# First norm's squares shared by two engines and summed on TensorE block by block, with the conditioning rows spread between them

## The chip, the cores and the metric

The kernel runs on one core of a Trainium2 chip. The metric is device time in microseconds (us) of one execution; of the kernel before there are three, with a median of 1330.14 us (1330.12 to 1335.97). A further execution was taken with the hardware profiler; all durations below come from it.

Engine names are those of the profile: PE is TensorE's matmul, PEld its weight load, DVE is VectorE, ACT is ScalarE, POOL is GpSimd, SP is SyncE, which here only issues DMAs. Each engine works through its own instructions in the order in which they were issued; engines wait for each other through semaphores.

## The reference

Two layers of a hybrid diffusion backbone: 256 latent tokens and 256 context tokens of width 1024. Each layer is an RMSNorm with a shift and a scale that depend on a conditioning vector, a combined projection into three token mixers, gates, a residual, a second such norm, a SwiGLU and a residual. What matters here is the beginning of the first layer:

```
silu_c, silu_cc = silu(c), silu(c_ctx)
mx = (silu_c @ w_ada[l] + b_ada[l])          # 6 rows of 1024: shift, scale, gate, ...
y = x * rsqrt(mean(x * x, axis=-1) + 1e-6) * g
h = y * (1 + scale) + shift                  # then h @ w_in
```

Every token needs the sum of 1024 squares before the first projection can begin. The context tokens use `silu_cc` in place of `silu_c`.

## The kernel before

All activations are kept transposed: eight tiles `h[0]` to `h[7]`, each 128 features (partitions) by 512 tokens (256 context, then 256 latent) in float32. They come in as four DMAs of two tiles each (`h_tiles`, L94). Weights come as a stream of 128x1024 blocks (`raw`, three buffers); ACT rounds each block to a high part and DVE computes the low part (L132, L122, tile `hl`), and every product is made of three matmuls (`mm3`, L204 to L206).

The order of the work is the order of the Python program: nothing is scheduled by a planner, and each engine's queue holds its instructions as the program issues them. The function that matters is `start()`. It does four things on the way to the first projection:

- **Conditioning rows (L483 to L489).** The two vectors `silu(c_ctx)` and `silu(c)` are spread over all partitions: 16 matmuls of 128x128 in float32 write four PSUM banks `outs[0..3]`, and `spread(i)` copies each bank into half of `cb[0]` or `cb[1]`. `cb` is used much later, by VectorE.
- **Norm sum (L491 to L502).** ACT squares each `h[k]` into a tile `sq` (four buffers), DVE adds it to `acc`, and when all eight are added four matmuls with a one-column operand (`acc` is the stationary side, `ones[:, 0:1]` the moving side) sum over the partitions: L502 writes four columns of bank `outs[4]`.
- **Shift and scale.** `nat_first(k)` multiplies the conditioning vectors with a block of weights (`wn`, L466), `nat_copy` takes the result out of PSUM, `nat_second(k)` turns it round (L476) and DVE makes the per-feature scale and shift `Ag` and `mods` (L477, L479).
- **Norm factor.** `norm_rstd` (L290 on ACT, L291, L292 and `newton` L272 to L274 on DVE) makes 1/rms, `norm_bcast` (L298) spreads it over the partitions into bank `outs[6]`, `mult` (L514) applies it, `mod` (L520 to L523) applies scale and shift and splits the result into `hn[k]`.

After that a loop over `k` runs seven output blocks per step (`block`, L531) on PE, with `nat_first(k + 1)` ahead of them.

In float32 the profile shows two passes for one matmul, each with its own weight load: the 16 matmuls of L486 are 32 instructions, the 4 of L502 are 8.

Of the kernel before, what the change touches and what calls it, by code (L numbers as in the profile page):

```python
# [12 lines left out]
AF = mybir.ActivationFunctionType  # L13
ALU = mybir.AluOpType
# [4 lines left out]
KT = 8  # L19
# [13 lines left out]
def hybrid_dit_kernel(ctx: ExitStack, tc: tile.TileContext, hT, wst, adaf, adan, vec_d,  # L33
                      bias_d, mask_d, dtab_d, rope_d, icnt_d, pw_d, out):
    nc = tc.nc
    V, S, P, TE = nc.vector, nc.scalar, nc.gpsimd, nc.tensor
# [10 lines left out]
    def pg():  # L47
        return pbank("g", 4)

    def pS():  # L50
        return pbank("s", 2)

    def pT():
        return pbank("t", 1)

    def pO():
        return pbank("o", 1)

    def tmp():
        return sm.tile([128, 512], F32, name="tmp", tag="tmp", bufs=3)  # L60
# [5 lines left out]
    ident = con.tile([128, 128], F32, name="ident")  # L66
    ones = con.tile([128, 64], F32, name="ones")
# [4 lines left out]
    cb = [con.tile([128, 1024], F32, name=f"cb{i}", tag=f"cb{i}") for i in range(2)]  # L72
# [11 lines left out]
    h = []  # L84
# [191 lines left out]
    def sqrt_table():  # L276
        S.activation(tiny(1, "dummy"), eps, AF.Sqrt)
# [10 lines left out]
    def norm_rstd(o, n):  # L288
        ms, sq, y = tiny(n, "ms"), tiny(n, "sq"), tiny(n, "rstd")
        S.activation(sq, o[:, :n], AF.Sqrt, bias=eps, scale=1.0 / D)  # L290
        V.tensor_scalar(ms, o[:, :n], 1.0 / D, 1e-6, op0=ALU.mult, op1=ALU.add)  # L291
        V.reciprocal(sq, sq)  # L292
        newton(y, sq, ms, n)
        return y

    def norm_bcast(y, tiles, R):
        for i, t in enumerate(tiles):
            TE.matmul(R[:, t * 128:(t + 1) * 128], y[:, i:i + 1].to_broadcast([128, 128]), ident,  # L298
                      start=True, stop=True)
        return R  # L300

# [7 lines left out]
    class Mod:  # L309
        def __init__(self, l, j, R, streams, share=True):  # L310
            self.a, self.t, self.k, self.share = (l, j, R, streams), None, 0, share

        def first(self, k):
            l, j, R, streams = self.a
            t = tmp()
            for s in streams:
                c = (CTX, X)[s]
                V.scalar_tensor_tensor(t[:, c], h[k][:, c], Ag[l][:, j, k, s:s + 1], R[:, c],
                                       op0=ALU.mult, op1=ALU.mult)
                b = mods[l][:, 24 * j + k, s:s + 1]  # L320
                if self.share and k % 2:
                    S.activation(t[:, c], t[:, c], AF.Identity, bias=b)
                    S.copy(hn[k][0][:, c], t[:, c])  # L323
                else:
                    S.activation(hn[k][0][:, c], t[:, c], AF.Identity, bias=b)  # L325
            return t
# [40 lines left out]
    def new_acc():  # L367
        return sm.tile([128, 512], F32, name="acc", tag="acc", bufs=1)
# [63 lines left out]
    def start():  # L432
        with tc.tile_pool(name="st", bufs=1) as sp:
# [4 lines left out]
            P.memset(ones, 1.0)  # L438
            S.activation(tiny(1, "dummy"), eps, AF.Silu)

            acc = new_acc()
            wn = {}

            def nat_load(k):
# [8 lines left out]
            csil = sp.tile([128, 8, 32], F32, name="csil")  # L453
# [6 lines left out]
            outs = [pg() for _ in range(4)] + [pS(), pS(), pT(), pO()]  # L460
            nat = outs[7]

            def nat_first(k):
                for kb in range(8):
                    g = slice(32 * (kb % 4), 32 * (kb % 4) + 32)
                    TE.matmul(nat[g, :256], csil[:, kb], wn[k][:, kb], start=(kb < 4), stop=(kb >= 4))  # L466

            def nat_copy():
                t = sp.tile([128, 256], F32, name="wt", tag="wt", bufs=2)
                V.tensor_copy(t, nat[:, :256])  # L470
                return t
# [8 lines left out]

            for s, off in enumerate((V_CC, V_C)):
                S.activation(csil[:, :, s], vec[:, off:off + 8], AF.Silu)
            for i in range(4):  # L483
                for b in range(4):
                    kb = 4 * (i % 2) + b
                    TE.matmul(outs[i][:, b * 128:(b + 1) * 128], csil[:, kb, i // 2:i // 2 + 1].to_broadcast([128, 128]),  # L486
                              ident, start=True, stop=True)
            def spread(i):
                S.copy(cb[i // 2][:, (i % 2) * 512:(i % 2) * 512 + 512], outs[i])  # L489

            for k in range(KT):  # L491
                t = sp.tile([128, 512], F32, name="sq", tag="sq", bufs=4)
                S.activation(t, h[k], AF.Square)
                if k == 0:
                    V.tensor_copy(acc, t)
                else:
                    V.tensor_tensor(acc, acc, t, op=ALU.add)
            sqrt_table()
            spread(0)
            o = outs[4]  # L500
            for i in range(4):
                TE.matmul(o[:, i:i + 1], acc[:, i * 128:(i + 1) * 128], ones[:, 0:1], start=True, stop=True)  # L502
            nat_first(0)
            y = norm_rstd(o, 4)
            for i in range(1, 4):
                spread(i)
            R = norm_bcast(y, range(4), outs[6])
            t0 = nat_copy()
            prep_to(0, True)
            Rs = sp.tile([128, 512], F32, name="Rs")  # L510
# [1 line left out]
            def mult(k):  # L512
                t = tmp()
                V.tensor_tensor(t, h[k], R if k == 0 else Rs, op=ALU.mult)  # L514
                return t
# [9 lines left out]
            t = mult(0)  # L525
# [8 lines left out]
            for k in range(KT):  # L534
# [3 lines left out]
                if more:  # L538
                    nat_first(k + 1)
                    prep_to(k + 1, True)  # L540
                    t = mult(k + 1)
# [688 lines left out]
    with tc.manual_schedule():  # L1230
        outs, u = start()
        with tc.tile_pool(name="mx0", bufs=1) as mp:
            ada_units(0, (2, 3, 4, 5), (0, 1))
            mixer(0, mp, outs, u)
        with tc.tile_pool(name="ff0", bufs=1) as fp:
            outs = out_ffn(0, fp)
        with tc.tile_pool(name="mx1", bufs=1) as mp:
            mixer(1, mp, outs, None)
        with tc.tile_pool(name="ff1", bufs=1) as fp:
            out_ffn(1, fp)  # L1240
# [119 lines left out]
```

## Time and profile before

| | |
|---|---|
| median of the runs | 1330.14 us |
| profiled execution, whole | 1340.45 us |
| its span on the core | 1338.7 us |
| PE busy | 1313.8 us (98%) |
| DVE busy | 850.1 us (64%) |
| ACT busy | 582.0 us (43%) |
| mean granted clock of PE | 0.99 |

The profiled execution is 10.31 us longer than the median of the others, so a difference is worked out against its 1340.45 us and then carried to the median. Busy shares are averages over the whole span. The change lies in the first 22 us, and there they say little: what counts is the chain of work that leads to the first projection. The profile's column for the granted clock has 1.00 for 2.4 GHz and 0.50 for 1.2 GHz; before the first recorded change of the clock it prints 1.00.

### The profile page before, as it was taken

The page shows a single profiled execution, that of the slowest core. Times are in us where ns is not written, and L with a number is a line of the kernel's source. Part 1 is how long each engine was busy: PE and PEld are TensorE (multiplying, and loading weights), DVE is VectorE, ACT ScalarE, POOL GpSimd, SP SyncE. Part 2 cuts the span into 40 slices and gives each one's busy share as a digit, 9 for nine tenths or more (in the row PEclk, how much of TensorE's full clock was granted, in tenths as well). Part 3 has the DMA queues.
Part 4 walks back from the last instruction along what each step waited for, and adds up shares of the span by engine and source line. Part 5 has one row for each costly group of instructions (what it writes and reads, how often), then busy time and mean ns, then how long its engine had stood idle before and what let it go on. Part 6 is the DMA issues. An engine that isn't in the chain of part 4 may idle for free.

```text
span 1338.7 us, 19983 instructions
## 1 busy us (share of the span) xinstructions
PE 1313.8 (98%) x7842; PEld 1145.4 (86%) x7842; DVE 850.1 (64%) x1445; ACT 582.0 (43%) x902; POOL 144.4 (11%) x213
## 2 busy tenths in 40 slices
PE   7999999999999999999999999999999999999997
PEld 6787777888888888888888888988889999999997
DVE  4487462877877666566565553665647887655554
ACT  4455555452232434222122232465567545643453
POOL 0034131111000010000000000152242200000000
PEclk7999999999999999999999999999999999999999
DMA  8433312443554514444445653142426775455552
GB/s 311 163 128 124 106 57 86 149 135 127 172 174 166 196 64 143 150 162 159 157 142 176 206 185 110 58 152 97 151 95 220 239 270 185 158 188 189 189 175 95
DMA packets 60141, 207.79 MB, mean 155 GB/s; under 512 B 6800, under 2 KB 11280, under 8 KB 59024
## 3 DMA queue, kind: packets, MB, share of 16 engines
q1 hardware_dynamic: 48528, 164.58, 36.4%
q10 hardware_dynamic: 11520, 41.95, 9.2%
q8 instruction: 61, 1.00, 0.3%
q14 instruction: 32, 0.26, 0.1%
HBM read 205.45 MB, written 1.05 MB: 154 GB/s over the span
## 4 chain that ended last, share of the span: by engine, by line
PE 86%; DVE 6%; ACT 4%; DMA 2%; issue 1%; SPq 0%; ACTq 0%; POOL 0%; DVEq 0%
PE pg L204 26%; PE pg L206 26%; PE pg L205 26%; DMA raw<-in_wst 1%; DVE hl L122 1%; ACT hl L132 1%; PE pt L687 1%; PE po L699 1%; PE po L909 1%; PE ps L656 1%; PE ps L655 1%; PE po L466 1%; DVE tmp L393 1%; DMA h<-in_hT 0%; ACT hn L325 0%
## 5 line engine op out<-in xcount | busy, mean ns | idle before, releaser
L204 PE MATMUL pg<-hn,hl 128*128 128x256 f32 (+1 forms) x1568 | 524.7, 335 | 2.7 <-ACT hn L325 1.1
L206 PE MATMUL pg<-hn,hl 128*128 128x256 f32 (+1 forms) x1568 | 520.5, 332 | 0.5 <-POOL hn L334 0.4
L205 PE MATMUL pg<-hn,hl 128*128 128x256 f32 (+1 forms) x1568 | 519.6, 331 | 0.9 <-DVE hl L122 0.9
L122 DVE TENSOR_TENSOR hl<-raw,hl 128x1024 fp32r<-128x1024 f32 (+1 forms) x277 | 342.8, 1243 | 157.8 <-ACT hl L132 157.0
L132 ACT CAST hl<-raw 128x1024 fp32r<-128x1024 f32 (+1 forms) x277 | 288.0, 1043 | 214.0 <-PE pg L206 98.1
L204 PEld LDWEIGHTS pg<-hn,hl 128*128 128x128 f32 x1568 | 296.4, 189 | 35.9 <-issue 3.8
L205 PEld LDWEIGHTS pg<-hn,hl 128*128 128x128 f32 x1568 | 297.8, 190 | 30.6 <-DVE hl L122 1.6
L206 PEld LDWEIGHTS pg<-hn,hl 128*128 128x128 f32 x1568 | 296.1, 189 | 30.7 <-POOL hn L334 1.5
L393 DVE CUSTOM_DVE_ANT_0 tmp<-ada,cb 128x1024 bf16<-128x1024 f32 x128 | 155.6, 1223 | 25.7 <-DMA ada<-in_adaf 19.1
L204 PE MATMUL pg<-fh,hl 128*128 128x256 f32 (+1 forms) x374 | 122.0, 326 | 0.0
L205 PE MATMUL pg<-fh,hl 128*128 128x256 f32 (+1 forms) x374 | 121.8, 326 | 0.0
L206 PE MATMUL pg<-fh,hl 128*128 128x256 f32 (+1 forms) x374 | 121.8, 326 | 0.0
L306 ACT CAST fh<-sg 128x512 fp32r<-128x512 f32 (+1 forms) x44 | 22.6, 514 | 139.8 <-DVE sg L1158 139.8
L334 POOL TENSOR_TENSOR hn<-tmp,hn 128x256 fp32r<-128x256 f32 x20 | 14.8, 741 | 621.5 <-ACT hn L323 364.3
L205 PEld LDWEIGHTS pg<-fh,hl 128*128 128x128 f32 x374 | 71.1, 190 | 6.0
L204 PEld LDWEIGHTS pg<-fh,hl 128*128 128x128 f32 x374 | 70.4, 188 | 6.1
L206 PEld LDWEIGHTS pg<-fh,hl 128*128 128x128 f32 x374 | 70.4, 188 | 6.0
L350 DVE SCALAR_TENSOR_TENSOR h<-pg,mods,h 128x256 f32<-128x256 f32 x72 | 32.7, 480 | 64.1 <-PE pg L206 63.9
L204 PE MATMUL pg<-naq,hl 128*128 128x512 f32 (+1 forms) x192 | 64.5, 336 | 0.2 <-ACT tmp L1014 0.2
L206 PE MATMUL pg<-naq,hl 128*128 128x512 f32 (+1 forms) x192 | 64.1, 334 | 0.0
L205 PE MATMUL pg<-naq,hl 128*128 128x512 f32 (+1 forms) x192 | 64.0, 333 | 0.0
L1158 DVE TENSOR_TENSOR sg<-pg,sg 128x512 f32<-128x512 f32 (+1 forms) x44 | 24.5, 557 | 49.5 <-PE pg L206 46.1
(239 smaller groups left out, 1449.3 us busy)
## 6 DMA issues: line engine op xcount, KB each, us to landing
raw<-in_wst SPq DMA_DIRECT2D x277, 512.0 KB, 3.8
ada<-in_adaf ACTq DMA_DIRECT2D x80, 512.0 KB, 4.1
wn<-in_adan SPq DMA_DIRECT2D x8, 1024.0 KB, 7.1
h<-in_hT SPq DMA_DIRECT2D x8, 512.0 KB, 6.0
bm<-in_bias SPq DMA_DIRECT2D x32, 128.0 KB, 2.0
out<-yt SPq DMA_DIRECT2D x4, 256.0 KB, 2.0
cs<-in_rope SPq DMA_DIRECT2D x2, 256.0 KB, 3.1
pw<-in_pw SPq DMA_DIRECT2D x2, 256.0 KB, 3.9
```

Of the source, the lines that this page charges most:

```text
L122: V.tensor_tensor(t[:, 1, c], r[:, c], t[:, 0, c].bitcast(F32), op=ALU.subtract)
L132: S.copy(t[:, 0, width(j)], r[:, width(j)])
L204: TE.matmul(o, wh, xh, start=a, stop=False)
L205: TE.matmul(o, wl, xh, start=False, stop=False)
L206: TE.matmul(o, wh, xl, start=False, stop=z)
L306: S.copy(d0, src)
L334: P.tensor_tensor(hn[k][1][:, c], t[:, c], hi, op=ALU.subtract)
L350: V.scalar_tensor_tensor(h[k][:, c], o, mods[l][:, col + k, s:s + 1], h[k][:, c], op0=ALU.mult, op1=ALU.add)
L393: V.tensor_tensor_reduce(out=tmp().bitcast(BF16), in0=tiles[n], in1=cb[s], scale=1.0, scalar=0.0, op0=ALU.mult, op1=ALU.add, accum_out=mod ...
L466: TE.matmul(nat[g, :256], csil[:, kb], wn[k][:, kb], start=(kb < 4), stop=(kb >= 4))
L655: TE.matmul(o, naq[hd][:, qc], nakd[hd][:, kc], start=True, stop=False)
L1158: V.tensor_tensor(e["s"][:, c], o, e["s"][:, c], op=ALU.mult)
```

## The change

Four things are different, all in `start()`:

1. The even `h[k]` are squared on ACT, the odd ones on DVE. There is no `acc` and no addition on DVE.
2. Each square is summed by its own four one-column matmuls, which accumulate over the eight blocks in `outs[4]`: 32 matmuls in place of 4.
3. The 16 matmuls that spread the conditioning vectors are no longer issued together: five come first, one after each block's sum, three after the last.
4. `cb[1]` is copied by DVE in place of ACT, and all four copies are issued behind `norm_bcast`.

```diff
-            acc = new_acc()
...
-            for i in range(4):
-                for b in range(4):
+            rows = [(i, b) for i in range(4) for b in range(4)]
+
+            def spread_mm(n):
+                for i, b in rows[:n]:
                     kb = 4 * (i % 2) + b
-                    TE.matmul(outs[i][:, b * 128:(b + 1) * 128], csil[:, kb, i // 2:i // 2 + 1].to_broadcast([128, 128]),
-                              ident, start=True, stop=True)
+                    TE.matmul(outs[i][:, b * 128:(b + 1) * 128],
+                              csil[:, kb, i // 2:i // 2 + 1].to_broadcast([128, 128]), ident, start=True, stop=True)
+                del rows[:n]
+
             def spread(i):
-                S.copy(cb[i // 2][:, (i % 2) * 512:(i % 2) * 512 + 512], outs[i])
-
+                c = cb[i // 2][:, (i % 2) * 512:(i % 2) * 512 + 512]
+                if i < 2:
+                    S.copy(c, outs[i])
+                else:
+                    V.tensor_copy(c, outs[i])
+
+            o = outs[4]
+            spread_mm(5)
             for k in range(KT):
                 t = sp.tile([128, 512], F32, name="sq", tag="sq", bufs=4)
-                S.activation(t, h[k], AF.Square)
-                if k == 0:
-                    V.tensor_copy(acc, t)
+                if k % 2:
+                    V.tensor_tensor(t, h[k], h[k], op=ALU.mult)
                 else:
-                    V.tensor_tensor(acc, acc, t, op=ALU.add)
+                    S.activation(t, h[k], AF.Square)
+                for i in range(4):
+                    TE.matmul(o[:, i:i + 1], t[:, i * 128:(i + 1) * 128], ones[:, 0:1],
+                              start=(k == 0 and i == 0), stop=(k == KT - 1 and i == 3))
+                spread_mm(1)
             sqrt_table()
-            spread(0)
-            o = outs[4]
-            for i in range(4):
-                TE.matmul(o[:, i:i + 1], acc[:, i * 128:(i + 1) * 128], ones[:, 0:1], start=True, stop=True)
+            spread_mm(3)
             nat_first(0)
             y = norm_rstd(o, 4)
-            for i in range(1, 4):
+            R = norm_bcast(y, range(4), outs[6])
+            for i in range(4):
                 spread(i)
-            R = norm_bcast(y, range(4), outs[6])
             t0 = nat_copy()
```

How this changes the queue of PE at the program's start, first as it was (`pg` are the banks of the spread vectors, `ps` the norm sum, `po` the shift and scale, `pt` the spread norm factor):

```order
L486 MATMUL pg_127<-ident_71,csil_121 128x128 x4
L486 MATMUL pg_128<-ident_71,csil_121 128x128 x4
L486 MATMUL pg_129<-ident_71,csil_121 128x128 x4
L486 MATMUL pg_130<-ident_71,csil_121 128x128 x4
L502 MATMUL ps_131<-ones_72,acc_108 128x1 x4
L466 MATMUL po_134<-wn_109,csil_121 32x256 x8
L298 MATMUL pt_133<-ident_71,rstd_194 128x128 x4
L476 MATMUL po_134<-sel_124,wt_209 128x2 x2
```

Here the sixteen spread matmuls stand together and four one-column matmuls follow. In the changed program the same stretch of PE's queue begins and ends so (the pair of an `L507` row and an `L487` row stands eight times in all, once for each square):

```order
L487 MATMUL pg_126<-ident_71,csil_120 128x128 x4
L487 MATMUL pg_127<-ident_71,csil_120 128x128
L507 MATMUL ps_130<-ones_72,sq_141 128x1 x4
L487 MATMUL pg_127<-ident_71,csil_120 128x128
L507 MATMUL ps_130<-ones_72,sq_148 128x1 x4
...
L507 MATMUL ps_130<-ones_72,sq_190 128x1 x4
L487 MATMUL pg_129<-ident_71,csil_120 128x128 x4
L465 MATMUL po_133<-wn_108,csil_120 32x256 x8
L298 MATMUL pt_132<-ident_71,rstd_212 128x128 x4
```

Between the first square and the shift-and-scale matmuls there are now 32 one-column matmuls and 11 spread matmuls, where there were 4 and none. On DVE, from the squares to the first `mult`, the changed queue is:

```order
L503 TENSOR_TENSOR sq<-h_92 128x512
L503 TENSOR_TENSOR sq<-h_94 128x512
L503 TENSOR_TENSOR sq<-h_96 128x512
L503 TENSOR_TENSOR sq<-h_98 128x512
L291 TENSOR_SCALAR ms<-ps 128x4
...
L274 SCALAR_TENSOR_TENSOR rstd<-nt,sq 128x4
L496 COPY cb_78<-pg 128x512 x2
L469 COPY wt<-po 128x256
L523 TENSOR_TENSOR tmp<-h_92,pt 128x512
```

The copy to `acc` and the seven additions are gone, and two copies of `cb[1]` stand ahead of `nat_copy` and `mult`.

## Rows read from the trace of the kernel before

**Rows 1.** The page: busy time of PE; the span in slices; the chain's shares

```profile
PE 1313.8 (98%) x7842; PEld 1145.4 (86%) x7842; DVE 850.1 (64%) x1445; ACT 582.0 (43%) x902; POOL 144.4 (11%) x213
...
PE   7999999999999999999999999999999999999997
...
PE 86%; DVE 6%; ACT 4%; DMA 2%; issue 1%; SPq 0%; ACTq 0%; POOL 0%; DVEq 0%
```

**Rows 2.** Chain of waits, 0 to 32 us: start us, us, what

```profile
9.36 0.70 DVE acc L497
...
11.75 0.70 DVE acc L497
...
12.50 1.87 PE ps L502 x8
14.37 1.86 PE po L466 x16
16.23 2.02 PE pt L298 x8
18.27 0.39 DVE tmp L514
...
21.17 0.50 PE pg L204
...
23.97 0.65 PE po L476 x4
...
27.38 0.43 PE ps L204
...
28.83 0.24 PE ps L205
```

**Rows 3.** Busy time by stretch; after POOL: granted clock, DMA share, GB/s

```profile
3.06:7.80 4.74, 4.74 (x22) 4.74 (x23) 1.81 (x3) 2.35 (x5) 0.00 (x0) 1.00 0.96 323
...
7.80:9.20 1.40, 1.39 (x12) 1.20 (x11) 0.69 (x1) 0.50 (x1) 0.00 (x0) 1.00 1.07 392
12.50:14.30 1.80, 1.80 (x9) 1.78 (x9) 0.00 (x0) 0.57 (x2) 0.00 (x0) 0.50 1.04 437
...
16.20:18.00 1.80, 1.80 (x12) 1.80 (x9) 0.42 (x1) 0.76 (x1) 0.00 (x0) 0.50 1.03 432
18.00:18.60 0.60, 0.59 (x6) 0.50 (x4) 0.33 (x1) 0.00 (x0) 0.00 (x0) 0.88 1.00 423
...
21.60:28.20 6.60, 6.60 (x19) 5.14 (x18) 3.88 (x8) 3.40 (x6) 0.00 (x0) 0.50 0.86 344
```

**Rows 4.** Timeline, 0 to 20 us: start us, us, instruction, idle before it

```profile
3.06 6.13 PE L486 MATMUL pg<-ident,csil 128*128 128x128 f32 x32 [3.06 <-ACT csil L482]
...
4.84 1.15 ACT L493 ACTIVATE sq<-h 128x512 f32<-128x512 f32 x2 [1.73 <-DMA h<-in_hT]
...
8.70 2.37 ACT L493 ACTIVATE sq<-h 128x512 f32<-128x512 f32 x4 [1.12 <-DMA h<-in_hT]
...
14.57 1.55 ACT L489 COPY cb<-pg 128x512 f32<-128x512 f32 x3
...
15.38 0.16 DVE L274 SCALAR_TENSOR_TENSOR rstd<-nt,sq 128x4 f32<-128x4 f32 x1
...
19.33 1.07 PE L466 MATMUL po<-wn,csil 128*32 128x256 f32 x16 [0.74 <-DVE mods L479]
```

**Rows 5.** Timeline at the program's end, the final norm at full clock

```profile
1330.07 0.36 PE L284 MATMUL ps<-ones,acc 128*128 128x1 f32 x2
...
1330.29 0.36 PE L284 MATMUL ps<-ones,tmp 128*128 128x1 f32 x2
...
1331.95 0.90 PE L298 MATMUL pt<-ident,rstd 128*128 128x128 f32 x4 [1.30 <-DVE rstd L274]
1332.89 0.42 DVE L1226 TENSOR_TENSOR yt<-yt,pt 128x256 f32<-128x256 f32 x1 [1.08 <-PE pt L298]
```

## The prediction

> **What bounds the kernel now.** I read the page first, then the chain of waits of the first 32 us, then the granted clock and the busy counts by stretch, then the timeline of PE, ACT and DVE over the first 20 us. The page says that PE is busy for 98% of the span, that only the first and the last of the 40 slices fall under nine tenths, and that 86% of the chain is PE [rows 1]. So once the projection blocks run, from 21.17 us on [rows 2], a later start is a later end: the loads, the rounding and the conditioning queues all hang on PE's progress and shift with it. The question is only when the first block starts and at which clock it runs.
>
> The chain to that start shows it [rows 2]: the last additions on DVE (0.70 us each, the last ending at 12.46), the eight one-column passes of L502 to 14.37, `nat_first` to 16.23, the spreading of the norm factor (L298) and its latency to 18.27, `mult`, scale and shift, and the block at 21.17. ACT and DVE lead up to 12.5; from there to 18.3 it is PE alone.
>
> Next, PE's rate. In 3.06 to 7.80 PE ran 22 passes in 4.74 us, 0.2155 us each; in 7.80 to 9.20 twelve in 1.39 us, 0.116 us each [rows 3]. The clock column prints 1.00 for both, but no change of clock had been recorded yet, and the passes say that the first stretch ran at half clock: L298, of the same shape, needs the same time at a printed 0.50 (eight passes, 2.02 us with the tail) [rows 2, 3]. The one-column passes are no cheaper. L502 needed 1.87 us for eight at 0.50 [rows 2], of which 1.78 us were weight loads [rows 3]: one column or 128, a pass lasts as long as its 128x128 load. At full clock the same form in the last norm takes 0.22 us for two [rows 5]. I use 0.2155 us at 1.2 GHz and 0.112 us at 2.4 GHz.
>
> **The change part by part.** *Removed:* the DVE additions behind the last square. The last pair of `h` allowed ACT's third square of its last four by 9.9 us (8.70 plus two times 2.37/4 [rows 4]). Shared by ACT at 0.59 us and DVE, the squares would end at about 10.6 in place of 12.46. A square on DVE does not occur in this stretch; a DVE addition of the same size is 0.70 us, ACT's square 0.59, and between 0.59 and 0.70 nothing changes below, because PE is late by far more. The most that this removal can give is 1.9 us.
>
> *Added on PE:* 28 more one-column matmuls, 56 passes, and 11 of the 16 spread matmuls, 22 passes, are moved behind the first square. Before, all 32 spread passes ran under the wait for the `h` loads, 3.06 to 9.19, and PE then stood idle to 12.50 [rows 2, 4]. That idle time of 3.3 us is the only cover for 78 passes, 16.8 us at the low clock.
>
> Step by step, with the clock low. Ten spread passes end at 3.06 + 10 x 0.2155 = 5.21. The first square (4.84 + 1.15/2 = 5.42 [rows 4]) releases PE at 5.45. From there PE never waits again: each block of features costs 8 + 2 passes, 2.15 us, and the squares come faster, also through four buffers, since square k + 4 only needs the sum of block k. Up to the end of the last sum stand 64 + 14 = 78 passes, 16.81 us, so PE reaches 22.26; L502's tail (14.37 - 12.50 - 8 x 0.2155 = 0.15) puts the sum at 22.4, against 14.37: 8.0 us later. Ahead of `nat_first` stand the last four spread matmuls, 8 passes, 1.72 us, to 23.98; before, `nat_first` followed at 14.37. That makes 9.6 us. The factor itself is ready at 22.4 + 1.17 (15.54 - 14.37, the end of L274 [rows 4]) = 23.6 and waits behind `nat_first` (1.86 us, to 25.84), as it did before. `mult` follows 9.6 us later than at 18.27, and so does the block.
>
> A small return: the clock's two recorded rises, at about 18.1 and 28.2 [rows 3], came 3.7 and 3.6 us after the last passes with one or two columns (the ends of L502 at 14.37 and of L476 at 24.62 [rows 2]), full-length work lying between. After 22.26 the same would put the rise near 25.9, where L298 begins: its 8 passes and 0.5 us of latency (1332.89 - 1331.95 less 4 x 0.112 [rows 5]) take 1.4 us in place of 2.02. I take 0.6 us back: **+9.0 us**.
>
> *DVE and ACT:* two copies of 128x512 move to DVE ahead of `nat_copy`. The trace has no such copy on DVE; ACT's takes 0.52 us (1.55/3 [rows 4]) and a DVE pass of that size 0.70, so 1.0 to 1.4 us. They can begin at 23.98 and end by 25.4, and `nat_copy` needs `nat_first`, 25.84: hidden, with 0.4 us to spare. Without that cover (PE at full clock) they would cost at most about 0.5 us. ACT's first cast moves behind two copies and is due only for the block. SP's load of the fourth `wn` waits for `nat_first(0)` to free its buffer and goes out some 9 us later; it is used two steps after that, and the queue, full up to then (DMA share 1.03 [rows 3]), is emptier. The three `wn` and `raw` already asked for land earlier relative to their use.
>
> *The clock of the first blocks:* before, they ran at 0.50 from 21.6 to 28.2, 0.43 us a pass against 0.24 later [rows 2, 3]; at full clock those 6.6 us would take 3.0 less. The approach to the block has the same sparse work as before (mult, scale, shift, a `nat_first` of 1.07 us [rows 4]), so I expect the same drop and count nothing: bounds -3.0 and +0.5 us (the first 0.43 us of the block were at full clock before).
>
> A rule to weigh against the row: the Trainium skill (TensorE: Matmul & The Clock Gate, section LDWEIGHTS) gives a load as columns over 1.2 GHz, 107 ns for 128. By that, the estimate for all 86 passes would be 9.2 us, and `nat_first` would begin at 14.6, 0.3 us later than before. The trace has twice that per float32 pass at the low clock; the measurement decides.
>
> Sum: 1340.45 + 9.0 = 1349.45 for the profiled kind of execution; the median of the others is 10.31 lower, so **1339.1 us**. Bounds of this case: passes at 0.2135 to 0.222 us (1.78/8) are -0.2 to +0.6; the return at L298 0 or 0.6; the blocks -3.0 to +0.5. Together +5.8 to +10.7, 1336 to 1341.
>
> **The rivals.** *A, the clock rises early, as before, near 7.9 us.* PE now has work from 3.06 to past 18 with one gap of 0.24 us, and steady work preceded the early rise before. The Trainium skill speaks for it too (same page, section Why this matters for your kernels): keeping TensorE continuously busy is its way to the full rate. Then 11.4 passes run by 7.9 and 74.6 x 0.112 = 8.4 us follow: 16.3; `nat_first` 1.07, L298 1.4, `mult` at 18.7, 0.45 us later than before. If the clock then also holds into the blocks, 3.0 come back: -2.6 to +0.5, 1327.5 to 1330.6, not slower. Against it: after 5.21 only one pass in five has 128 columns, where before every pass did; and in 21.6 to 28.2 PE was occupied throughout and still at 0.50, with two-column passes in the middle. It decides from a rise at about 7 us for no loss at all, or 13 us if the blocks gain 3.0.
>
> *B, the clock rises partway through the sums,* at x between 8 and 22: each us of delay costs 0.48, so +0.45 + 0.48 (x - 7.9), less up to 3.0: 1330 to 1336. For it: the rise at 18.1 had 1.87 us of one-column passes in the work before it. The loss is over 6.65 us, 0.5% of the time, only from x above 20.8.
>
> *C, the sums vanish behind the loads* and the shorter chain of squares counts: at most -1.9, with -3.0 in the blocks -4.9, 1325.2. It needs 70 passes in the time from 5.45 to 10.6, 0.074 us each, which no row shows.
>
> **How the numbers follow.** Forecast case 0.73, B 0.13, A 0.12, C 0.02. What a measurement of this kernel can tell from no change is about 0.5%, 6.65 us: 1323.5 to 1336.8. A gain of that size is beyond even C's bound; I leave 0.02 for it. The forecast case lies below 1336.8 only with the blocks at full clock, 0.04 of its 0.73: slower 0.69, same 0.29. The range of 1331 to 1341 us takes in nearly all of the forecast case and most of B.
>
> **What would show it.** Right: one-column passes of some 0.21 us from 5.5 to 22 us in pairs with spread passes, PE without a wait between; a clock of 0.50 up to about 26; `mult` near 27 and the first block near 30; ACT and DVE idle between squares, their buffers waiting for PE. Wrong: passes of 0.11 us before 22, a sum that ends before 16, or PE waiting for squares. A right start with a time below 1336 would mean that the first blocks ran at full clock, or that the delay is caught up later by something that this profile does not show as idle on PE.

## The result, and the profile after

The changed kernel took 1346.56 us (median of six, 1341.04 to 1349.37) against 1333.22 us of the kernel before beside it (six, 1330.12 to 1338.75): a ratio of 1.0089 with a 95% interval of 1.0064 to 1.0114, slower. The forecast was 1339.1 us, 1.0067 of 1330.14, in a range of 1331 to 1341 us. The direction came as forecast, the time lies outside the range.

Executions of either kernel fall into two groups some 6.5 us apart, and four of the six of the changed kernel (1346.55 to 1349.37 against 1341.04 and 1342.06) but three of the six of the kernel before (1335.97 to 1338.75 against 1330.12 to 1330.48) are in the upper one. What differs between the groups lies in the second layer and is shown below.

The profiled execution of the changed kernel has 1346.55 us (span 1344.7). Its page has the lines of [rows 1] so:

```profile
PE 1323.9 (98%) x7898; PEld 1156.4 (86%) x7898; DVE 847.0 (63%) x1443; ACT 579.3 (43%) x896; POOL 145.1 (11%) x213
...
PE   8999999999999999999999999999999999999997
...
PE 91%; DVE 4%; ACT 3%; issue 1%; DMA 1%; POOL 0%; ACTq 0%; DVEq 0%
```

The 56 passes more are there (7898 - 7842), and the first slice is fuller. The chain has 91% PE in place of 86, but this is no sign of the change: five points of the span are some 67 us, far more than the start holds, and a later profile of the same changed kernel has 87% where three of the kernel before have 88%. The chain of waits of the first 37 us (start us, us, what), for [rows 2]:

```profile
3.08 2.50 PE pg L487 x10
5.58 1.62 PE ps L507 x8
7.21 0.64 PE pg L487 x2
7.84 1.50 PE ps L507 x8
...
20.64 1.50 PE ps L507 x8
22.14 1.92 PE pg L487 x8
24.05 1.86 PE po L465 x16
25.92 1.65 PE pt L298 x8
...
27.60 0.38 DVE tmp L523
...
30.49 0.50 PE pg L204
30.99 0.23 PE pg L205
...
36.28 1.00 PE po L465 x16
```

From 3.08 us to L298 the chain is PE without a break. A block's sum and its spread matmul repeat every 2.13 us (7.84, 9.97, ...), ten passes of 0.2134 us. `mult` begins at 27.60 in place of 18.27 and the first block at 30.49 in place of 21.17: 9.3 us later. But the blocks then run at 0.23 us a pass, not at 0.43 [rows 2], and the L465 of the third block of features (the third `nat_first`) begins at 36.28, where L466 began at 29.99 in the first profile of before: 6.3 us. The difference of the two profiled executions, 1346.55 - 1340.45, is 6.1. In that first profile the third and the fourth `nat_first` are these rows of the chain:

```profile
29.99 1.00 PE po L466 x16
...
36.48 1.00 PE po L466 x16
```

The clock by stretch, for [rows 3] (after POOL: granted clock, DMA share, GB/s):

```profile
9.00:12.00 3.00, 3.00 (x16) 3.00 (x16) 0.69 (x1) 0.56 (x2) 0.00 (x0) 1.00 1.00 412
...
32.00:34.00 2.00, 2.00 (x12) 1.64 (x11) 1.30 (x4) 0.76 (x2) 0.00 (x0) 1.00 1.01 401
```

The 1.00 of the first line is again the value printed before the first recorded change: 16 passes in 3 us (one or two counted at either edge) are the half-clock rate of [rows 3], as the period of 2.13 us says more exactly.

The timeline of DVE and ACT has the waits that were forecast:

```profile
11.56 0.63 ACT L505 ACTIVATE sq<-h 128x512 f32<-128x512 f32 x1 [2.44 <-PE ps L507]
...
13.64 0.69 DVE L503 TENSOR_TENSOR sq<-h 128x512 f32<-128x512 f32 x1 [3.57 <-PE ps L507]
...
24.09 0.69 DVE L496 COPY cb<-pg 128x512 f32<-128x512 f32 x1 [0.18 <-PE pg L487]
...
25.99 0.43 DVE L469 COPY wt<-po 128x256 f32<-128x256 f32 x1 [1.20 <-PE po L465]
```

The last square is ready at 14.3 us and waits for a buffer before that, while its sum comes at 20.6: the squares are never what PE waits for. The two copies on DVE (0.68 and 0.69 us) end 1.2 us before `nat_copy` can begin.

### The profile page after: what moved, and what is told of

It reads as the page before. It is cut to its first block, busy times and chain, and to the rows that moved or that the text cites. A ratio compares the mean times of both kernels' runs of the same rounds, so it can differ in the third digit from the quotient of the medians.

```text
span 1344.7 us, 20081 instructions
## 1 busy us (share of the span) xinstructions
PE 1323.9 (98%) x7898; PEld 1156.4 (86%) x7898; DVE 847.0 (63%) x1443; ACT 579.3 (43%) x896; POOL 145.1 (11%) x213
## 3 DMA queue, kind: packets, MB, share of 16 engines
HBM read 205.45 MB, written 1.05 MB: 154 GB/s over the span
## 4 chain that ended last, share of the span: by engine, by line
PE 91%; DVE 4%; ACT 3%; issue 1%; DMA 1%; POOL 0%; ACTq 0%; DVEq 0%
PE pg L204 27%; PE pg L206 27%; PE pg L205 27%; PE po L918 1%; PE pt L696 1%; PE po L708 1%; DVE hl L122 1%; PE ps L507 1%; ACT hl L132 1%; PE ps L665 1%; PE ps L664 1%; PE pg L487 1%; PE po L465 1%; ACT hn L325 0%; DVE tmp L318 0%
```

## The experiments

Ratios are against the kernel before on the same chip in the same series, with 95% intervals. In the expectations, "the second step's matmuls (36.48 us in the first profile)" are the fourth `nat_first`, 6.49 us after the one at 29.99 us.

**The kernel before, profiled again.**

> The kernel before, unchanged, profiled once more. Theory P (the delay is PE's passes at half clock, and the one profiled execution of before that I worked from had an unusually slow start): its ratio to itself is 1.000 within 0.004; if this execution is one of the shorter ones (near 1330 us), its first blocks run at full clock and the second step's shift-and-scale matmuls (36.48 us in the first profile) start near 31 to 33 us. Rival L (the extra loss of the measurement lies later in the kernel): the start is as in the first profile, 36.5 us, also in a short execution, and the difference to 1340 us appears behind it.

Ratio 0.9993 (0.9968 to 1.0017). The profiled execution has 1332.76 us, and its fourth `nat_first` begins at 35.03 us, only 1.45 us ahead of the first profile:

```profile
12.09 1.05 PE ps L502 x8
...
28.54 1.00 PE po L466 x16
...
35.03 1.00 PE po L466 x16
```

So 6.2 of the 7.7 us between these two executions of one program lie later. As rival L has it, something behind the start counts: PE's passes in the second layer's feed-forward part. Two more executions were profiled.

> The kernel before once more, one profiled execution. The page of the first profile (1340.45 us) had lost 6.4 us against another execution (1332.76 us) in the feed-forward part of the second layer, where a pass took 0.1176 us in place of 0.1132, and 1.5 us at the start. Theory P2 (three independent states: the clock at the start, the clock at the second layer's norm, the pass time behind it): an execution near 1329.5 us has passes of 0.1132 us and its first blocks at full clock, with the second step's matmuls of the shift and scale at 31 to 33 us. Rival: it starts at 35 to 36.5 us like the two profiled ones, and the 3 us between 1332.8 and 1329.5 lie elsewhere.

> The same as the run ahead of it, a further execution: P2 as there; a time near 1336 would have passes of 0.1176 us in the second layer's feed-forward part.

They have 1329.32 and 1336.71 us. Their chains of waits, first the one of 1329.32:

```profile
12.07 1.05 PE ps L502 x8
13.12 1.23 PE po L466 x16
14.35 2.08 PE pt L298 x8
16.46 0.68 DVE tmp L514
...
25.50 1.00 PE po L466 x16
...
32.00 1.00 PE po L466 x16
```

and the one of 1336.71:

```profile
11.70 1.07 PE ps L502 x8
...
25.29 1.00 PE po L466 x16
...
31.78 1.00 PE po L466 x16
```

The starts are alike, and 4.5 us ahead of the first profile (29.99 - 25.50). Of this, 1.8 us are there at `mult` (16.46 against 18.27): the norm sum begins 0.4 us earlier and takes 1.05 us, at full clock, in place of 1.87, and `nat_first` takes 1.23 in place of 1.86 [rows 2]. The other 2.7 us come in the first blocks, which run at half clock for a shorter time. The 7.4 us between the two are in the second layer. Busy time from 1200 to 1240 us, the execution of 1329.32 first, then that of 1336.71:

```profile
1200.00:1240.00 40.00, 40.00 (x355) 40.00 (x355) 23.25 (x27) 16.37 (x19) 0.00 (x0) 1.00 0.58 192
```

```profile
1200.00:1240.00 40.00, 40.00 (x342) 40.00 (x341) 22.21 (x27) 15.62 (x18) 0.00 (x0) 1.00 0.57 189
```

At the same clock, one has 355 passes in 40 us and the other 342; start to start it is 0.1132 and 0.1176 us. Over the 180 us of the second layer's feed-forward part that is 6 to 7 us. The first profile of before and the profile after both have 342. Two of P2's three parts are seen here: the start and this pass time vary, and not together. The third is not: at the second layer's norm the clock falls in all four profiles of before (to 0.50 from 1134 to 1138 us in these two, from 1138 to 1142 us in the other two).

**All spread matmuls first.** The edit:

```diff
-            spread_mm(5)
+            spread_mm(16)
...
-                spread_mm(1)
...
-            spread_mm(3)
```

> The changed kernel with all 16 spread matmuls ahead of the sums, as before: PE has 32 passes at 3.06 and then 64 one-column passes without a break. Theory P with one-column passes that do not hold the clock: the clock rises near 8 us as before, falls within some 3 us of the last spread pass, and the last sum ends between 18 and 23 us, 4 to 8 us after the 14.4 of before; time about 1.004 to 1.009 of before. Rival H (one-column passes hold a clock that is already up): 64 passes at 0.112 us, the last sum at 16.4 to 17, the first blocks at full clock, time 0.998 to 1.003 of before. Rival L: the time stays at 1.009 whatever the start does.

Ratio 1.0047 (1.0015 to 1.0080). The chain, and below it the clock by stretch:

```profile
9.51 11.15 PE ps L507 x64
20.66 1.86 PE po L465 x16
...
33.75 1.00 PE po L465 x16
```

```profile
9.60:11.00 1.40, 1.40 (x15) 1.40 (x14) 0.00 (x0) 0.62 (x1) 0.00 (x0) 1.00 0.97 407
12.00:13.00 1.00, 1.00 (x6) 1.00 (x7) 0.00 (x0) 0.77 (x2) 0.00 (x0) 0.50 1.03 434
18.00:19.00 1.00, 1.00 (x6) 1.00 (x7) 0.00 (x0) 0.00 (x0) 0.00 (x0) 0.50 1.02 410
```

This shows the mechanism most plainly. The clock is up when the one-column passes begin at 9.51, and while PE does nothing but these, without a pause, it falls, by 12 us, and stays at 0.50. PE's busy column reads 100% throughout. Rival H, that such passes hold a clock that is up, is refuted by this profile. The last sum ends at 20.66, inside the expectation.

**Half of the sums.** The sums of the even blocks are left out, so the norm rests on half of the features:

```diff
-                for i in range(4):
+                for i in range(4) if k % 2 else ():
...
-                              start=(k == 0 and i == 0), stop=(k == KT - 1 and i == 3))
+                              start=(k == 1 and i == 0), stop=(k == KT - 1 and i == 3))
```

> The changed kernel with the sums of the four even blocks left out (the norm then rests on half of the features): 32 passes fewer, nothing else. Theory P: 32 x 0.2135 = 6.8 us less on PE before the factor, the last sum at 15.2 to 15.5 us in place of 22.1, the first block near 23.7 in place of 30.5, time 1.003 to 1.005 of before. Rival L: the same 6.8 us, but from a remaining excess: 1.004 to 1.006. Rival N (PE is not the limit of the sums, the squares are): the last sum stays later than 18 us.

Ratio 1.0026 (1.0000 to 1.0051); the last sum ends at 12.54 us and the first block begins at 20.39, 10.1 us ahead of the changed kernel where 6.8 were expected. The chain says why:

```profile
5.99 1.00 PE ps L507 x8
...
7.55 0.79 PE ps L507 x8
8.33 0.55 PE pg L487 x4
8.89 0.94 PE ps L507 x8
...
10.89 1.64 PE ps L507 x8
```

In this execution the clock rose: the first sum takes 1.00 us where eight passes at half clock take 1.71, the second and third 0.79 and 0.94, the fourth, with the clock down again, 1.64. None of the three theories had that, so the pass count alone was too simple an account. What raised the clock is not shown. The rise lies within the first sum, when PE had run twelve spread passes in place of ten and the doubled share of spread passes between the sums had not yet begun; and this mix did not hold the clock, which printed 0.50 from 9.75 to 16 us. The ten times, 1329.63 to 1340.34 us, spread wider than the two groups alone, so the rise need not have come in every execution; one was profiled.

**One sum, with shared squares.** The changed kernel with the spread matmuls first, the squares added on DVE and summed once; the sharing and the moved copies stay:

```diff
+            acc = new_acc()
...
-            spread_mm(5)
+            spread_mm(16)
...
-                for i in range(4):
-                    TE.matmul(o[:, i:i + 1], t[:, i * 128:(i + 1) * 128], ones[:, 0:1],
-                              start=(k == 0 and i == 0), stop=(k == KT - 1 and i == 3))
-                spread_mm(1)
+                if k == 0:
+                    V.tensor_copy(acc, t)
+                else:
+                    V.tensor_tensor(acc, acc, t, op=ALU.add)
...
-            spread_mm(3)
+            for i in range(4):
+                TE.matmul(o[:, i:i + 1], acc[:, i * 128:(i + 1) * 128], ones[:, 0:1], start=True, stop=True)
```

> The changed kernel with its squares shared by ACT and DVE and its copies moved, but with the spread matmuls first and the squares added on DVE and summed once, as before. Theory P2 (the sums block by block and the spread matmuls behind them are the whole loss): the loss of 1.008 is gone; what is left is DVE, which now makes four squares besides the eight additions and copies: six operations of 0.7 to 0.8 us behind the third pair of tiles in place of four additions, so the norm sum starts 0.3 to 1 us later than before, 1.000 to 1.001. Rival (sharing the squares or moving the copies costs by itself): 1.003 or more.

Ratio 1.0017 (0.9993 to 1.0041). What is left of the loss cannot be told from no change. In the profile the norm sum begins at 13.92 us against 11.70 to 12.50 before, 1.4 to 2.2 us later and more than expected: DVE, which squares and adds, is most of the chain from 5.74 on, and the sum then runs at half clock:

```profile
13.92 1.87 PE ps L513 x8
...
29.21 1.00 PE po L466 x16
```

The third `nat_first`, at 29.21, is 3.7 us behind the 25.50 of the execution of before with 1329.32 us. So most of the loss is the sums block by block with the spread matmuls among them. The rival, that sharing the squares costs 1.003 or more by itself, is not excluded by an interval up to 1.0041; but its cost, DVE's queue, is not on the changed kernel's chain, where PE goes from sum to sum without a wait.

**Fillers that hold the clock.** From what the first two profiles showed of the clock, the kernel before was given 12 more dense matmuls behind the spread ones and 3 behind the first `nat_second`, into a bank not yet used:

```diff
+            def fill(n):
+                for b in range(n):
+                    TE.matmul(outs[5][:, :128], csil[:, b % 8, 0:1].to_broadcast([128, 128]), ident, start=True, stop=True)
+
+            fill(12)
...
             nat_second(0, t0)
+            fill(3)
```

> The kernel before with 12 more 128-column matmuls behind the 16 spread matmuls (in PE's idle time from 9.2 to 12.5 us) and 3 behind the first scale-and-shift matmuls, into an unused bank. Theory P: the clock that rose near 8 us is held, the norm sum, the spread factor and the first blocks run at full clock, and the second step's shift-and-scale matmuls start 3 to 5.5 us before the 36.48 of the first profile; against typical executions of before, if those already start fast, 0.997 to 1.000. Rival L: the time does not change, 1.000. If the clock is not up at 9 us the fillers cost up to 2 us: 1.0015.

Ratio 0.9985 (0.9960 to 1.0010). The norm sum takes 1.07 us, L298 1.17, and the fourth `nat_first` begins at 30.71 us, 5.8 ahead of the first profile and 1.1 to 1.3 ahead of the two executions that start alike:

```profile
14.30 1.17 PE pt L298 x8
...
30.71 1.00 PE po L466 x16
```

The same was then done around the second layer's norm as well (`fill(6)` ahead of its norm sum, `fill(9)` behind it, `fill(6)` behind `norm_bcast`).

> The kernel before with fillers at both norms on which PE runs dry: at the start as in the filler run, and 6 + 9 + 6 matmuls of 128 columns around the norm sum of the second layer's second norm, into an unused bank. Theory P2: the clock does not fall at 1137 us either, some 2 to 3 us less there; with the start's 2 to 3, 0.995 to 0.997. If the pass time of 0.1176 us comes from the fall of the clock at that norm, it no longer occurs and the times do not split: no execution over 1330. Rival: the fillers delay the norm sum by as much as they gain, and the pass time is drawn independently: 0.998 to 1.000, with some executions 6 us above the others.

Ratio 0.9980 (0.9954 to 1.0006). The clock no longer falls at that norm; busy time from 1136 us on, this kernel first, then the kernel before:

```profile
1136.00:1140.00 4.00, 4.00 (x35) 3.94 (x34) 2.26 (x6) 3.83 (x8) 2.03 (x3) 1.00 0.00 0
1140.00:1144.00 4.00, 3.46 (x30) 3.25 (x29) 2.91 (x4) 3.48 (x5) 0.00 (x0) 1.00 0.50 146
```

```profile
1140.00:1144.00 4.00, 4.00 (x19) 3.98 (x20) 3.57 (x9) 3.63 (x9) 1.92 (x3) 0.50 0.00 0
```

But its times still split, eight from 1327.07 to 1329.46 and four from 1333.85 to 1336.05. It was timed once more.

> The kernel before with fillers at both norms, timed again to narrow the interval of its first run (0.998, 0.9954 to 1.0006). P2: the clock is held at both norms, the second-layer pass time is still drawn per execution: 0.997 to 0.999, with one execution in three some 6 us above the others. Rival (the fillers gain nothing): 1.000.

Ratio 1.0001 (0.9978 to 1.0024): four executions from 1326.73 to 1328.14, eight from 1333.67 to 1335.10. This profile has 342 passes in 1200 to 1240 us, the one of the run before it 355, both with the clock held at that norm. So the longer pass time in the second layer does not need the fall of the clock there, and with eight of twelve executions in the upper group a gain of one or two us cannot be told. Whether the fillers are worth anything is not settled; they are no version of which it can be said that it beats the kernel before.

**The changed kernel, again.**

> The changed kernel, unchanged, timed again. Theory P2: its start is always slow (last sum at 22.1 us, since the passes keep the clock low), so against a typical before it loses 22.14 + 0.15 - 14.4 and 1.9 for the spread passes, 9.5 us, plus 1 to 2 where before starts at full clock: 1.007 to 1.009. Rival: the 1.0089 of the first measurement was chance in the pass time of the second layer (4 of 6 executions had it), and the ratio is now 1.004 to 1.006.

Ratio 1.0079 (1.0055 to 1.0103), with 1339.75 to 1342.11 us in seven of ten. The profiled execution (1339.75 us) has the shorter pass time in the second layer (356 passes from 1200 to 1240 us), and the same start:

```profile
20.94 1.50 PE ps L507 x8
...
24.35 1.48 PE po L465 x16
25.84 1.10 PE pt L298 x8
26.96 0.38 DVE tmp L523
...
35.70 1.00 PE po L465 x16
```

Against the execution of before with 1329.32 us, which has the shorter pass time too: `mult` 26.96 against 16.46 (10.5 us), the third `nat_first` 35.70 against 25.50 (10.2 us), the whole 10.4 us. That is the change's cost, from one profile of each, and all of it is in the first 27 us. The median of this series, 1340.62 us, lies inside the range of the prediction; seven of the sixteen executions of the changed kernel in the two series have the longer time, and whether the change has a part in how often that comes is not shown.

## Why the prediction was wrong

*Right: the passes.* 78 passes of 0.2155 us to 22.26 and 8 more to 23.98 were forecast; it was 22.14 and 24.05. `mult` was put 9.0 us later and came 9.3 later than in the same profile. That the clock would stay low under one-column passes, against rival A, held in each of the two profiles after, and the run with the spread matmuls first shows it by itself. So did the return, L298 at 1.65 and 1.10 us where 1.4 were forecast, though the clock rose at points some 2 us apart in the two profiles. Removing the additions gave nothing, the DVE copies were hidden, and nothing later changed by more than 0.2 us (10.2 us at the third `nat_first`, 10.4 in the whole). Rivals B and C did not come about.

*Wrong, 3.0 us: "I expect the same drop and count nothing", the term for the clock of the first blocks.* After its late rise the clock stayed up through the blocks: 0.23 us a pass from 30.99 us [rows 2 has 0.43]. I had this as a bound. Against the profile I worked from it turns +9.3 into +6.3.

*Wrong, 4.5 us the other way: the step from 1340.45 us to the median, with the start of the execution that I took as the base.* I carried the sum to the median by subtracting 10.31 us, as if all of that were common to both kernels. That execution had parts of its own: some 6 us were the pass time of the next point, and 4.5 us were the start: the norm sum at half clock, and the first blocks at half clock for longer. All three later profiles of before have the norm sum at full clock (1.05 to 1.07 us); the third `nat_first` begins at 25.3 and 25.5 us in two of them and at 28.54 in the other, not at 29.99. The changed kernel did not have that advantage in either of its profiles: its clock was low until 22 us. So the change costs 10.2 to 10.5 us against the execution with 1329.32 us, not 9.0 and not 6.3. That 9.0 comes so near is partly luck: the gain in the blocks and the base's slow start nearly cancel. The rows of clock in one profile [rows 3] were one draw of something that differs between executions.

*Not in the prediction at all, 6.5 us: the pass time in the second layer.* 0.1176 in place of 0.1132 us, in some executions of either kernel. By their times, the median of three that I forecast from came from two executions without it, and four of the six after had it. 1330.1 (the lower group of before in that series) + 10.4 + 6.5 = 1347.0, against a measured median of 1346.56. Of the 7.5 us by which the forecast was missed, some 6 are this and some 1.4 the cost itself, 10.4 in place of 9.0. The 6 are the luck of six executions: in the second series, with three of ten, they are absent from the median.

The range failed for these reasons: its ends came from mechanisms of the change alone, and the spread of the kernel before (1330.12 to 1335.97 in three runs) was not in it.

## What to carry to other kernels

Count a float32 matmul with one column as its weight load, 0.21 us a pass at half clock, however small its result, and do not put such work where it takes the place of dense matmuls: it kept PE busy and the clock down. Before a reduction is moved from an engine with time to spare (DVE, 0.7 us for a block) to the engine that bounds the kernel, work out the price of a block there, here 1.71 us (eight passes). And where a profiled execution is far from the median, look for what it had of its own, in a second profile, before carrying a difference over.

## What the runs showed of the hardware

- The clock fell under PE at 100% busy: with 64 one-column passes back to back it was at 1.00 up to 11 us and at 0.50 in 12 to 13 us, and did not rise while they lasted. In the changed kernel no rise came between 5 and 22 us. The Trainium skill (TensorE: Matmul & The Clock Gate, What's actually happening) states that the clock is set by how busy PE has been recently; the busy column, at 100% here, does not tell that. The Trainium skill's advice to keep TensorE continuously busy (same page, Why this matters for your kernels) was met here by that column and did not bring the full rate.
- The column of the granted clock prints 1.00 until the first recorded change; in the changed kernel the pass times up to 22 us say 0.50 (0.2134 us a pass, against 0.11 to 0.12 at full clock).
- At the same printed clock of 1.00, 128x256 passes ran at 0.1132 or 0.1176 us for the whole of the second layer's feed-forward part, 355 or 342 passes in 40 us, and it differed between executions of one program. The fall of the clock at the norm ahead of it is not needed for either (both occur with the clock held). What decides between them stays open.
